# Contrast adjustment on one Trainium2 core: the means moved from ScalarE to VectorE and TensorE, tiles moved as whole rows, and the first store held until the fifth load

## The chip, the core and the metric

The kernel runs on one core of a Trainium2 chip. The core has five engines that run side by side: TensorE (PE in the profile), VectorE (DVE), ScalarE (ACT), GpSimd (POOL) and SyncE (SP). Data move between the memory (HBM) and the on-chip SBUF by 16 DMA engines; a transfer is issued by an instruction on an engine's queue, here SP for loads and ACT for stores. The metric is the device time of one execution in microseconds (us); lower is better.

## What is computed

`x` holds 16 x 3 images of 512 x 512 numbers in f32, 50.33 MB; the output has the same shape. Each image is stretched around its own mean by a factor of 1.5 and clipped to 0..1.

```python
def reference(x, factor):
    mean = np.mean(x, axis=(2, 3), keepdims=True)
    return np.clip(mean + factor * (x - mean), 0, 1).astype(np.float32)
```

An image has to be read as a whole before its first output number is known. The kernel writes `mean + factor * (x - mean)` as `factor * x + bias`, with `bias = (1 - factor) * mean`.

## The kernel before

The input is cut into 12 tiles of 128 partitions by 8192 columns (4.19 MB each). One row of 8192 numbers is 32 KB, an image fills 32 rows, so a tile holds four whole images. The tiles go through `ring`, an SBUF buffer with six places (`BUFS`): tile t uses place t % 6, is loaded into it, clipped in place, and stored from it. Tile t + 6 can be loaded into the place only when the store of tile t has read it out.

The order on each engine is the program's order: the main block runs under a manual schedule, and what is planned on one engine stays in the sequence in which it is written. Semaphores between engines and transfers are set by the framework from the tiles that are read and written.

Per tile:
- `load` (L74, on SP's queue) brings it in. Tiles 0 and 1 come alone, tiles 2 and 3 in one transfer, tiles 4 and 5 in one transfer; from tile 6 on they come one by one, each issued behind the store of the tile six before it.
- `add` (L89, ScalarE) copies the tile onto itself and sums each row into a column of `sums`. A table has to be loaded for it once. For tile 0 the sum is divided: ScalarE sums columns 4352 to 8191, VectorE the first 4352 (L108).
- `shift_by` (L94, TensorE) multiplies `sums` with `blockw`, a 128 x 128 matrix of four 32 x 32 blocks filled with (1 - factor) / pixels. One matmul with one column adds the 32 rows of each image and leaves the bias in every row of a PSUM tile, `bias`.
- `clip` (L78 and L82, VectorE) does `x * factor + bias`, and then max with 0 and min with 1, two instructions over the tile.
- `store` (L99, on ACT's queue) writes it out. Tile 0 is clipped and stored in three pieces of 1024, 2048 and 5120 columns (`CUTS`), so that stores can begin early; the others go as one transfer.

The loop sets what stands behind what on ACT's queue: the sum of tile t + 1 is written ahead of the store of tile t.

```python
        for t in range(1, n_tiles):
            shift_by(t, own)
            clip(t, 0, ROW)
            if t + 1 < n_tiles:
                own = add(t + 1)
            store(t, 0, ROW)
            if t + BUFS < n_tiles:
                load(t + BUFS)
```

Of the kernel before, what the change touches and what calls it, by code (L numbers as in the profile page):

```python
# [1 line left out]

# [4 lines left out]


P = 128  # L10
ROW = 8192
BUFS = 6
CUTS = (0, 1024, 3072, ROW)
SUM = 4352


@with_exitstack
def kernel(
    ctx: ExitStack,
    tc: tile.TileContext,  # L20
    x: bass.AP,
    factor: float,
    out: bass.AP,
):

    nc = tc.nc
    f32 = mybir.dt.float32
    Alu = mybir.AluOpType  # L30
    Act = mybir.ActivationFunctionType

    B, C, H, W = x.shape
    n_img, n_pix = B * C, H * W
    ppi = n_pix // ROW
    per_tile = P // ppi
    n_tiles = n_img // per_tile
    assert ppi * ROW == n_pix and per_tile * n_tiles == n_img

    factor = float(factor)  # L40
    wconst = (1.0 - factor) / float(n_pix)

    x_f = x.rearrange("b c h w -> (b c h w)")
    out_f = out.rearrange("b c h w -> (b c h w)")

    def dram(ap, t, c0=0, c1=ROW):
        return bass.AP(tensor=ap.tensor, offset=t * P * ROW + c0, ap=[[ROW, P], [1, c1 - c0]])

    consts = ctx.enter_context(tc.tile_pool(name="consts", bufs=1))
    xpool = ctx.enter_context(tc.tile_pool(name="xpool", bufs=1))  # L50
    small = ctx.enter_context(tc.tile_pool(name="small", bufs=1))
    psum = ctx.enter_context(tc.tile_pool(name="psum", bufs=1, space=bass.MemoryType.PSUM))


    sums = small.tile([P, 2 * n_tiles], f32, name="sums")
    bias = psum.tile([P, n_tiles], f32, name="bias")

    blockw = consts.tile([P, P], f32, name="blockw")
    nc.gpsimd.memset(blockw, 0.0)  # L59
    for a in range(0, P, ppi):  # L60
        nc.gpsimd.memset(blockw[a : a + ppi, a : a + ppi], wconst)  # L61


    ring = xpool.tile([P, BUFS, ROW], f32, name="ring")

    def load(t, c0=0, c1=ROW, n=1):

        b = t % BUFS
        src = bass.AP(
            tensor=x_f.tensor,  # L70
            offset=t * P * ROW + c0,
            ap=[[ROW, P], [P * ROW, n], [1, c1 - c0]],
        )
        nc.sync.dma_start(out=ring[:, b : b + n, c0:c1], in_=src)  # L74

    def clip(t, c0, c1):
        part = ring[:, t % BUFS, c0:c1]
        nc.vector.tensor_scalar(  # L78
            out=part, in0=part, scalar1=factor, scalar2=bias[:, t : t + 1],
            op0=Alu.mult, op1=Alu.add,  # L80
        )
        nc.vector.tensor_scalar(  # L82
            out=part, in0=part, scalar1=0.0, scalar2=1.0, op0=Alu.max, op1=Alu.min
        )

    def add(t, c0=0):
        part = ring[:, t % BUFS, c0:ROW]
        own = sums[:, 2 * t : 2 * t + 1]
        nc.scalar.activation(out=part, in_=part, func=Act.Copy, accum_out=own)  # L89
        return own  # L90

    def shift_by(t, *parts):
        for k, part in enumerate(parts):
            nc.tensor.matmul(  # L94
                bias[:, t : t + 1], blockw, part, start=k == 0, stop=k == len(parts) - 1
            )

    def store(t, c0, c1):
        nc.scalar.dma_start(out=dram(out_f, t, c0, c1), in_=ring[:, t % BUFS, c0:c1])  # L99

    with tc.manual_schedule():
        load(0)
        load(1)
        load(2, n=2)
        load(4, n=2)

        rest = sums[:, 1:2]
        nc.vector.tensor_reduce(  # L108
            out=rest, in_=ring[:, 0, 0:SUM], axis=mybir.AxisListType.X, op=Alu.add
        )  # L110
        shift_by(0, add(0, SUM), rest)
        for c0, c1 in zip(CUTS[:-2], CUTS[1:-1]):
            clip(0, c0, c1)
            store(0, c0, c1)
        clip(0, CUTS[-2], ROW)
        own = add(1)
        store(0, CUTS[-2], ROW)
        load(BUFS)
        for t in range(1, n_tiles):
            shift_by(t, own)  # L120
            clip(t, 0, ROW)
            if t + 1 < n_tiles:
                own = add(t + 1)
            store(t, 0, ROW)
            if t + BUFS < n_tiles:
                load(t + BUFS)


# [1 line left out]
_INS = ['x', 'factor']  # L130
_OUTS = [((16, 3, 512, 512), 'float32')]

_NUMBERS = {'factor': 1.5}


# [26 lines left out]
```

## Time and profile before

| | us |
|---|---|
| median of 3 runs | 239.19 (239.05 to 239.28) |
| the profiled execution: its span, first to last instruction | 237.8 |
| around the span (median less span) | 1.4 |
| VectorE busy | 112.1 |
| ScalarE busy | 82.9 |
| TensorE busy | 7.6 |

The page gives the profiled execution by its span; its time outside of the span isn't given apart, and the row around the span compares it with the median of the runs. The kernel reads 50.33 MB and writes 50.33 MB, 423 GB/s over the span.

Lines of the profile are read so: in the slices, the span is cut into 40 equal parts and each digit is the busy share of a part in tenths. A group has its line in the kernel, engine, operation, output <- input with partitions x columns and type, how often; then the busy time and the mean ns of one; then the idle time of the engine ahead of them and who ended it. A wait line has who waited for whom, us in total, times, and the longest. In a window the engines stand in the order PE, PEld (weight loads), DVE, ACT, POOL, each with busy us and instructions, then the granted TensorE clock, the busy share of the DMA engines and GB/s. The trace also keeps a record of each packet that a DMA engine moved: queue, start, duration and bytes; one row of a tile is one packet.

### The profile page before, as it was taken

What the parts mean: (1) busy time and instruction counts of PE and PEld (TensorE: products, weight loads), DVE (VectorE), ACT (ScalarE), POOL (GpSimd) and SP (SyncE); (2) the same over time, 40 slices, a digit from 0 to 9 for tenths busy, and PEclk for the clock granted to TensorE, in tenths of its full rate; (3) what the DMA queues carried; (4) which work ended last, traced back from release to release, by engine and by line L of the source; (5) the groups of instructions that cost most, each with busy time, mean ns of one, the idle gap of its engine ahead of it and who ended that gap; (6) DMA issues with size and microseconds to landing.
All of it is one profiled execution on the core that took longest, in us unless ns stands there. A gap on an engine that the chain in (4) does not pass through costs nothing.

```text
span 237.8 us, 219 instructions
## 1 busy us (share of the span) xinstructions
PE 7.6 (3%) x26; PEld 6.5 (3%) x26; DVE 112.1 (47%) x29; ACT 82.9 (35%) x25; POOL 0.9 (0%) x9
## 2 busy tenths in 40 slices
PE   0010000000000000000000000000000000000000
PEld 0000000000000000000000000000000000000000
DVE  0078786009990039979407705902920950770000
ACT  2051900399000697380091083056038009100000
POOL 1000000000000000000000000000000000000000
DMA  7999999999999999999999999999999999999996
GB/s 265 441 441 442 401 471 429 391 413 430 457 441 435 413 408 430 435 435 441 441 441 441 441 435 435 402 419 430 435 441 441 441 441 441 441 430 413 413 430 259
DMA packets 3712, 100.66 MB, mean 423 GB/s; under 512 B 384, under 2 KB 384, under 8 KB 512
## 3 DMA queue, kind: packets, MB, share of 16 engines
q1 hardware_dynamic: 1696, 50.33, 49.6%
q10 hardware_dynamic: 2016, 50.33, 49.1%
HBM read 50.33 MB, written 50.33 MB: 423 GB/s over the span
## 4 chain that ended last, share of the span: by engine, by line
DMA 52%; another core or an unknown queue 15%; DVE 11%; issue 9%; PE 1%; ACT 1%; SPq 0%; ACTq 0%
DMA ring<-in_x_dram 33%; DMA out_dram<-ring 20%; DVE ring L78 6%; DVE ring L82 6%; PE bias L94 1%; ACT ring L89 1%; SPq L74 0%; ACTq L99 0%; ACTq L89 0%
## 5 line engine op out<-in xcount | busy, mean ns | idle before, releaser
L89 ACT ACTIVATE ring<-ring 128x8192 f32<-128x8192 f32 (+1 forms) x12 | 80.7, 6725 | 119.4 <-DMA ring<-in_x_dram 119.4
L78 DVE TENSOR_SCALAR ring<-ring,bias 128x8192 f32<-128x8192 f32 (+3 forms) x14 | 54.3, 3880 | 87.1 <-PE bias L94 87.1
L82 DVE TENSOR_SCALAR ring<-ring 128x8192 f32<-128x8192 f32 (+3 forms) x14 | 53.4, 3817 | 0.5
L94 PE MATMUL bias<-sums,blockw 128*128 128x1 f32 x26 | 7.6, 361 | 196.1 <-ACT ring L89 195.6
L94 PEld LDWEIGHTS bias<-sums,blockw 128*128 128x128 f32 x26 | 6.5, 311 | 197.1 <-ACT ring L89 179.9
L108 DVE TENSOR_REDUCE sums<-ring 128x1 f32<-128x4352 f32 x1 | 4.7, 4686 | 13.0 <-DMA ring<-in_x_dram 13.0
L89 ACT ACTIVATION_READ_ACCUMULATOR ring<-ring 128x1 f32 x12 | 2.2, 186 | 0.0
L89 ACT ACT_TABLE_LOAD x1 | 1.3, 1283 | 0.7 <-PEq L143 0.7
L61 POOL MEMSET blockw<- 32x32 f32 x4 | 0.5, 116 | 0.2
L59 POOL MEMSET blockw<- 128x128 f32 x1 | 0.2, 205 | 0.3 <-POOLq L143 0.3
L143 POOL MEMSET const-bfloat16-1.0<- 128x1 bf16 x1 | 0.1, 111 | 0.0
L143 POOL MEMSET const-uint8-127<- 128x1 uint8 x1 | 0.1, 111 | 0.0
L143 POOL MEMSET const-float32-1.0<- 128x1 f32 x1 | 0.1, 108 | 0.0
L143 POOL MEMSET const-float32-0.0<- 128x1 f32 x1 | 0.1, 103 | 0.2 <-issue 0.2
## 6 DMA issues: line engine op xcount, KB each, us to landing
out_dram<-ring ACTq DMA_DIRECT2D x11, 4096.0 KB, 44.2
ring<-in_x_dram SPq DMA_DIRECT2D x8, 4096.0 KB, 33.3
ring<-in_x_dram SPq DMA_DIRECT2D x2, 8192.0 KB, 60.6
out_dram<-ring ACTq DMA_DIRECT2D x1, 2560.0 KB, 37.5
out_dram<-ring ACTq DMA_DIRECT2D x1, 1024.0 KB, 25.9
out_dram<-ring ACTq DMA_DIRECT2D x1, 512.0 KB, 16.1
```

Of the source, the lines that this page charges most:

```text
L59: nc.gpsimd.memset(blockw, 0.0)
L61: nc.gpsimd.memset(blockw[a : a + ppi, a : a + ppi], wconst)
L78: nc.vector.tensor_scalar(out=part, in0=part, scalar1=factor, scalar2=bias[:, t : t + 1], op0=Alu.mult, op1=Alu.add,)
L82: nc.vector.tensor_scalar(out=part, in0=part, scalar1=0.0, scalar2=1.0, op0=Alu.max, op1=Alu.min)
L89: nc.scalar.activation(out=part, in_=part, func=Act.Copy, accum_out=own)
L94: nc.tensor.matmul(bias[:, t : t + 1], blockw, part, start=k == 0, stop=k == len(parts) - 1)
L108: nc.vector.tensor_reduce(out=rest, in_=ring[:, 0, 0:SUM], axis=mybir.AxisListType.X, op=Alu.add)
L143: nc = _bacc.Bacc("TRN2", target_bir_lowering=False, num_devices=1)
```

## The change

- ScalarE computes nothing and loads no table. Its queue has the 12 stores only.
- `head` (VectorE) sums the first 4096 columns of a tile into `sums`. `shift` (TensorE) multiplies `blockw` with the other 4096 columns in eight matmuls of 512 columns, all accumulated in one PSUM tile `acc` (two buffers), and adds the product with `sums` to its first column. VectorE then sums `acc` over its 512 columns into `bias`, now in SBUF.
- Every tile is loaded and stored as one transfer of 128 rows of 32 KB. SP's first six instructions are the loads of tiles 0 to 5, with no wait.
- Tile 0 is clipped up to column 7680, then tile 1 is summed and clipped. Then VectorE sums the first 512 columns of tile 4 (`begun`), for which it must wait until the fifth load has landed, and only then clips the last 512 columns of tile 0. The store of tile 0 waits for that piece, and the other stores follow it on the same queue.
- From then on, each turn of the loop sums and clips tile t on VectorE and TensorE, stores it, and issues the load of tile t + 6.

The core of the diff:

```diff
-CUTS = (0, 1024, 3072, ROW)
-SUM = 4352
+BLK = 512
+HEAD = 4096
...
-    bias = psum.tile([P, n_tiles], f32, name="bias")
+    bias = small.tile([P, n_tiles], f32, name="bias")
...
+    def head(t, k=0, c0=0, c1=HEAD):
+        own = sums[:, 2 * t + k : 2 * t + k + 1]
+        nc.vector.tensor_reduce(
+            out=own, in_=ring[:, t % BUFS, c0:c1], axis=mybir.AxisListType.X, op=Alu.add
         )
+        return own
...
+    def shift(t, *heads):
+
+        acc = psum.tile([P, BLK], f32, name="acc")
+        for c0 in range(HEAD, ROW, BLK):
+            nc.tensor.matmul(
+                acc, blockw, ring[:, t % BUFS, c0 : c0 + BLK], start=c0 == HEAD, stop=False
+            )
+        for own in heads:
+            nc.tensor.matmul(acc[:, 0:1], blockw, own, start=False, stop=own is heads[-1])
+        nc.vector.tensor_reduce(
+            out=bias[:, t : t + 1], in_=acc, axis=mybir.AxisListType.X, op=Alu.add
+        )
...
-    def add(t, c0=0):
-        part = ring[:, t % BUFS, c0:ROW]
-        own = sums[:, 2 * t : 2 * t + 1]
-        nc.scalar.activation(out=part, in_=part, func=Act.Copy, accum_out=own)
-        return own
+    with tc.manual_schedule():
+        for t in range(BUFS):
+            load(t)
...
+        gate = BUFS - 2
+        shift(0, head(0))
+        clip(0, 0, ROW - BLK)
+        shift(1, head(1))
+        clip(1)
+        begun = head(gate, 0, 0, BLK)
+        clip(0, ROW - BLK, ROW)
+        for t in range(n_tiles):
+            if t == gate:
+                shift(t, begun, head(t, 1, BLK, HEAD))
+            elif t > 1:
+                shift(t, head(t))
+            if t > 1:
+                clip(t)
+            store(t)
             if t + BUFS < n_tiles:
                 load(t + BUFS)
```

More of the change, by code (lines that the diff above doesn't have):

```diff
@@ L30 @@
     Alu = mybir.AluOpType
-    Act = mybir.ActivationFunctionType
     B, C, H, W = x.shape
@@ L37 @@
     n_tiles = n_img // per_tile
-    assert ppi * ROW == n_pix and per_tile * n_tiles == n_img
+    assert ppi * ROW == n_pix and per_tile * n_tiles == n_img and n_tiles > BUFS
     factor = float(factor)
@@ L44, with dram @@
     out_f = out.rearrange("b c h w -> (b c h w)")
-    def dram(ap, t, c0=0, c1=ROW):
-        return bass.AP(tensor=ap.tensor, offset=t * P * ROW + c0, ap=[[ROW, P], [1, c1 - c0]])
+    def dram(ap, t):
+        return bass.AP(tensor=ap.tensor, offset=t * P * ROW, ap=[[ROW, P], [1, ROW]])
     consts = ctx.enter_context(tc.tile_pool(name="consts", bufs=1))
@@ L51 @@
     small = ctx.enter_context(tc.tile_pool(name="small", bufs=1))
-    psum = ctx.enter_context(tc.tile_pool(name="psum", bufs=1, space=bass.MemoryType.PSUM))
+    psum = ctx.enter_context(tc.tile_pool(name="psum", bufs=2, space=bass.MemoryType.PSUM))
     sums = small.tile([P, 2 * n_tiles], f32, name="sums")
-    bias = psum.tile([P, n_tiles], f32, name="bias")
+    bias = small.tile([P, n_tiles], f32, name="bias")
     blockw = consts.tile([P, P], f32, name="blockw")
@@ L64, with load, store, clip @@
     ring = xpool.tile([P, BUFS, ROW], f32, name="ring")
[L66 to L72, printed above, removed]
-        )
-        nc.sync.dma_start(out=ring[:, b : b + n, c0:c1], in_=src)
-    def clip(t, c0, c1):
+    def load(t):
+        nc.sync.dma_start(out=ring[:, t % BUFS, :], in_=dram(x_f, t))
+    def store(t):
+        nc.scalar.dma_start(out=dram(out_f, t), in_=ring[:, t % BUFS, :])
+    def head(t, k=0, c0=0, c1=HEAD):
+        own = sums[:, 2 * t + k : 2 * t + k + 1]
+        nc.vector.tensor_reduce(
+            out=own, in_=ring[:, t % BUFS, c0:c1], axis=mybir.AxisListType.X, op=Alu.add
+        )
+        return own
[10 more added lines that the diff above has]
+        )
+    def clip(t, c0=0, c1=ROW):
         part = ring[:, t % BUFS, c0:c1]
@@ L84, in clip @@
         )
-    def add(t, c0=0):
-        part = ring[:, t % BUFS, c0:ROW]
-        own = sums[:, 2 * t : 2 * t + 1]
-        nc.scalar.activation(out=part, in_=part, func=Act.Copy, accum_out=own)
-        return own
[L92 to L99, printed above, removed]
-    with tc.manual_schedule():
[L102 to L124, printed above, removed]
+    with tc.manual_schedule():
+        for t in range(BUFS):
[15 more added lines that the diff above has]
+            store(t)
             if t + BUFS < n_tiles:
```

## The prediction

> **What bounds the kernel now.** I read the page from the slices (part 2) to the chain (part 4) and the groups (part 5), then the waits by engine, busy time in chosen windows, the timeline, and last the trace's records of single DMA packets.
>
> ```profile
> span 237.8 us, 219 instructions
> ...
> PE 7.6 (3%) x26; PEld 6.5 (3%) x26; DVE 112.1 (47%) x29; ACT 82.9 (35%) x25; POOL 0.9 (0%) x9
> ...
> DMA  7999999999999999999999999999999999999996
> ...
> DMA packets 3712, 100.66 MB, mean 423 GB/s; under 512 B 384, under 2 KB 384, under 8 KB 512
> ...
> DMA 52%; another core or an unknown queue 15%; DVE 11%; issue 9%; PE 1%; ACT 1%; SPq 0%; ACTq 0%
> ```
>
> No engine is busy for half of the span, and the DMA row is 9 in every slice but the two at the ends. The 26% that the chain gives to DVE, issue, PE and ACT is a path through the waits; transfers run beside all of it. So the kernel is bound by 100.66 MB and by the rate at which the 16 DMA engines take it.
>
> ```profile
> 5.00:20.00 15.00, 1.14 (x4) 1.00 (x4) 6.28 (x4) 3.50 (x2) 0.00 (x0) 1.00 1.00 433
> ```
>
> This is the busy time in a window of pure loading (after the times: PE, PEld, DVE, ACT, POOL, granted clock, DMA share, GB/s). 433 GB/s is a plateau: by packet records spread over their durations, 5 us bins give 432 to 434 for pure loads (5 to 25 us), loads and stores mixed (55 to 195) and pure stores (195 to 235). A 32 KB packet takes 1.213 us (median), and each DMA engine has 50.33 x 2 MB / 16 / 32768 B = 192 of them to carry: 192 x 1.213 = 232.9 us. The first packet starts at 1.76, the last ends at 236.64, and 1.1 us follow. So on the engine that ends last, 234.9 - 232.9 = 2.0 us are all that a change of order can win. A bubble, in which neither queue has a packet, is all that it can newly lose.
>
> Those 2.0 us, from the packet records (sums over 16 engines, divided by 16):
> - the opening packets, 1.6 to 2.06 us in place of 1.213: 0.58 us. They stay.
> - short rows of the first tile's three stores: 4 KB packets take 0.159 us, 8 KB 0.309, 20 KB 0.761. Per engine 8 x (0.159 + 0.309 + 0.761) = 9.83 against 8 x 1.213 = 9.70: 0.13 us.
> - some 60 load packets of 1.24 to 1.85 us, nearly all starting between 35 and 54 us: 0.71 us. The bins there are 417, 422, 420, 409 GB/s. Elsewhere after the opening such packets cost 0.04 us in all.
> - one engine falls behind in that stretch and stays there: at the end 15 engines stop by 235.88 and the last at 236.64, 0.76 later. After the second load its lag was 0.05.
> (Packets overlap slightly, 16.05 in flight, which gives back some 0.6.)
>
> **The change part by part.** All prices below are against the profiled span of 237.8 us. The median of the runs is 239.19, so 1.4 us lie around the span; I carry these 1.4 over.
>
> ```profile
> L89 ACT ACTIVATE ring<-ring 128x8192 f32<-128x8192 f32 x11 | 77.3, 7027 | 108.4 <-DMA ring<-in_x_dram 108.4
> L78 DVE TENSOR_SCALAR ring<-ring,bias 128x8192 f32<-128x8192 f32 x11 | 49.4, 4490 | 86.4 <-PE bias L94 86.4
> L82 DVE TENSOR_SCALAR ring<-ring 128x8192 f32<-128x8192 f32 x11 | 48.7, 4427 | 0.4
> L94 PE MATMUL bias<-sums,blockw 128*128 128x1 f32 x26 | 7.6, 361 | 196.1 <-ACT ring L89 195.6 <-DVE sums L108 0.5
> ...
> L108 DVE TENSOR_REDUCE sums<-ring 128x1 f32<-128x4352 f32 x1 | 4.7, 4686 | 13.0 <-DMA ring<-in_x_dram 13.0
> ```
> ```profile
> SPq L74 <- DMA out_dram<-ring: 157.5, 8, 33.3
> ```
>
> The groups with shapes kept apart give the unit prices; the last line, from SP's waits, says that loads from the seventh on wait for stores to land.
>
> 1. ScalarE's sums go: 7.03 + 0.19 us a tile, and the table load of 1.28 us. None was on the DMA's path, as the transfers ran beside them: worth 0. Stores no longer queue behind an ACTIVATE on ACT: store 1, ready at 39.5, was issued at 45.65 because the sum of tile 2 (waiting for the joint load of 2 and 3) stood ahead. Other transfers were in flight, so that too is 0.
>
> 2. VectorE gets 4096 columns of sum: 4686 / 4352 = 1.077 ns a column, 4.4 us. It also gets a 512-column sum from PSUM, not in this trace: nearest row 512 x 1.077 = 0.55, ends 0.5 and 1.2; I take 0.6. With the two clips (8.92) and the small matmul's 0.6 between, 14.6 us a tile when data wait. A tile needs 8.39 MB / 433 = 19.4 us of DMA. Spare, 4.8 us a tile: cost 0.
>
> 3. TensorE gets eight 128x512 f32 matmuls a tile, of which no row exists. Each f32 matmul shows as two records; the pair with one column takes 0.59, which sets a floor of 8 x 0.59 = 4.7 us. The nearest row in columns is the weight load: two of 128 columns start 0.167 us apart, 1.3 ns a column. At that pace 512 columns in two records take 1.34 us, a tile 10.7; if each record passes its columns twice, 21.4. I take 10.7, the value with no further assumption, and keep 4.7 and 21.4.
> The Trainium skill prices it otherwise: its page FP8 and Floating Point Precision (TensorE Precision Notes) gives true f32 four passes, and TensorE: Matmul & The Clock Gate (Part 1) gives 2.4 GHz warm and 1.2 GHz after idling. An estimate from both is 8 x 4 x 512 columns = 6.8 us warm, 13.7 cold; the sum comes out the same by either. No row here shows such a matmul, and the granted clock of 1.00 stands beside an almost idle PE.
>
> 4. The gate. Loads 0 to 5 are issued at once; at 433 GB/s each takes 9.7 us, landing at 12.7, 22.4, 32.1, 41.8, 51.5, and the sixth, if alone, at 61.2. VectorE and TensorE do tiles 0 and 1 meanwhile: sum 0 by 24.9 (13.0 + 10.7 + 0.6 + 0.6), the first 7680 columns' clip (8.4) to 33.3, head 1 to 37.7, its matmul and reduction to 38.9, clip 1 to 47.9. The added wait is on VectorE, `begun`, for load 4. Behind it stand the last 512 columns of tile 0's clip (2 x 0.46, from 757 and 1285 ns for 1024 and 2048 columns), all of tiles 2 to 11, and so store 0 and every store behind it on ACT's queue. It ends at 51.8 + 0.6 + 0.9 = 53.3. The cover is load 5: until 61.2 the DMA has work without any store, 7.9 us of cover. The first store before showed its first packet 3.6 us after its issue, behind loads in flight; so store 0 starts at 57 and nothing is idle. Without the cover each us of delay would cost one.
>
> 5. After it. Load 5 and store 0 share the rate until 65.4, store 0 lands at 71, and load 6 starts some 2 us later. Store 1 waits on ACT's queue from 53.4, and store 2 is ready at 67.6 (head 4.4, 1.2, clip 8.9 after 53.3), so stores run alone at 433 meanwhile, as they did from 195 us on. From there VectorE offers a store each 14.6 us and the queue takes one each 19.4, so a store always waits; load t+6 needs store t landed, and load 7 is issued near 88 while load 6 runs to 94. Loads end near 191 (before 194.3), the last tile is ready at 191 + 10.7 + 1.2 + 8.9 = 212, and its turn on the queue comes at 225: 13 us spare.
>
> 6. Whole rows. The short-row loss of 0.13 goes. The slow packets have one trait that I can use: they lie where small-row stores met the two-tile loads. Whole-row stores beside single-tile loads, from 78 us on, lost under 0.03 us in 116. That is the nearest row for the new mixture, so I let the 0.71 go. Its bounds are 0 won and 0.71 won. Of the lagging engine's 0.76, which arose with them, I take 0.3, ends 0 and 0.76.
>
> Sum: 0.13 + 0.71 + 0.3 = 1.1 us. Span 237.8 - 1.1 = 236.7, time 239.19 - 1.1 = **238.1**. The ends: gains from 0.1 to 1.6, 237.6 to 239.1.
>
> **Rivals.**
> (a) The slow packets come whatever the rows: the 4 KB packets ran from 23 to 34 us without them, and 20 KB packets from 55 to 64 too, which speaks for another cause, such as the first mixing of reads and writes. Then only 0.13 is won, less what the new mixture loses: 239.1, from 238.7 to 239.6. The Trainium skill has a rule that would leave as little: HBM Reference, Specifications, puts a core alone near 425 GB/s, and the kernel's mean is 423. The trace disagrees, with 433 for 15 us in a row.
> (b) TensorE becomes the bound, the case on the slower side. Its place is the eight matmuls ahead of each bias, its price x us a tile. The last tile's store would be issued at 13 + 12 x + 10.7 (small matmul, PSUM sum, clip), and end some 11.7 later (9.7 of packets, 2 of start and finish): 35.4 + 12 x. It reaches 237.8 at x = 16.9; below that nothing shows, at 18 the span is 251.4 and the time 252.8, at 21.4 the time is 294. The gate's cover ends near the same x: store 0 goes out at 13 + 2x + 11.8, so past 61 from x = 18. For it: 21.4 is within my bounds; against it: that needs two passes at the slow pace with nothing overlapped.
> (c) The whole mixed stretch runs like 35 to 54, because TensorE's 2 MB of reads a tile or the one-tile queues slow the packets: 0.71 us per 19 over 55 to 191 is 5.1, so 239.19 - 1.1 + 5.1 = 243.2. Against it, ScalarE read and wrote whole tiles before, with no such packets after 61 us.
>
> **How the numbers follow.** Forecast 0.57, (a) 0.23, (b) 0.10, (c) 0.10. 0.2% is 0.5 us, about what a measurement of this kernel can tell. The forecast's own range is 237.6 to 238.6. Faster: 0.56, nearly all of the forecast. Same: 0.20, most of (a). Slower: 0.24, (b), (c) and the rest of (a). The range of 237.5 to 240 holds the forecast and (a), and leaves out (b) and (c), 0.20 together.
>
> **What would show it.** Right: bins near 433 from 5 us to the end, 16 packets in flight throughout, store 0 issued at 53 to 54 and load 6 at 71 to 73, no load packet group above 1.24 us, DVE ahead of the stores from 80 us on. Wrong: a DMA slice under 9 near 60 us (gate), PE busy above 17 us a tile (b), GB/s bins of 410 to 425 (a, c), or an engine whose last packet ends well after the others.

## The result and the profile after

The changed kernel takes 240.33 us (median of 6 runs), the kernel before 239.12 (median of 6): a ratio of 1.006, interval 1.0046 to 1.0074. It is slower by some 1.2 us, where 1.1 faster was forecast, so 2.2 us lie between the predicted 238.1 and the measured time.

The page of the changed kernel; the rows answer to those shown of the kernel before, and PEclk is the granted clock of TensorE in tenths of full speed.

```profile
span 238.4 us, 594 instructions
...
PE 113.8 (48%) x218; PEld 49.7 (21%) x218; DVE 167.8 (70%) x51; POOL 0.9 (0%) x9
...
PEclk9999975865685988979687589569559659855555
DMA  7999999999999999999999999999999999999995
GB/s 269 440 434 440 440 440 429 434 434 357 434 423 434 434 429 412 440 443 434 440 434 434 429 434 429 434 429 429 423 434 440 440 440 429 434 440 429 429 440 220
DMA packets 3457, 100.68 MB, mean 422 GB/s; under 512 B 384, under 2 KB 384, under 8 KB 384
...
q8 instruction: 1, 0.02, 0.0%
```

The DMA is still full from end to end, at the same mean rate. Two things are new. The tenth slice has 357 GB/s, and a third queue, q8, moved one packet of kind "instruction", 0.02 MB. TensorE's row suggests what is fetched: 218 matmul and 218 weight-load records, where there were 26 of each. I call such a packet, which brings instructions while the program runs, a refill.

In the packet records (as in the prediction, lost time is summed over the 16 engines and divided by 16):

| us | before | after |
|---|---|---|
| first packet starts | 1.76 | 1.74 |
| opening packets, lost an engine | 0.58 | 0.70 |
| load packets slowed near the first stores, lost an engine | 0.71 (35 to 54 us) | 1.03 (54 to 57 us) |
| short rows, lost an engine | 0.13 | 0 |
| mean end of the 16 engines | 235.75 | 236.18 |
| end of the last engine | 236.64 | 237.19 |
| instruction packets after the start | none | 16 KB at 106.28 for 0.88 us, and at 239.31 |

The packet at 106.28 occupies one of the 16 DMA engines. The load packet that starts at 107.16 behind it takes 1.753 us in place of 1.213. Together 0.88 + 0.54 = 1.42 us fall on that one engine. Joining each packet to the one that ends where it starts gives each of the 16 engines its 192 rows. By these chains the engine of the refill was 0.28 us ahead of the mean of the 16 before it, 1.05 behind after it, and 1.02 behind at the end: the lag isn't made up. It ends at 237.19, and the second-last engine at 236.61. So 0.58 of the 1.42 us reach the end of the run; nearly all of the rest, 0.81, is what that engine had been ahead of the one that was last until then.

The gate, in windows of the changed kernel (columns PE, PEld, DVE, POOL, granted clock, DMA share, GB/s) and in its timeline:

```profile
50.00:54.00 4.00, 0.00 (x0) 0.00 (x0) 2.04 (x4) 0.00 (x0) 0.50 0.99 426
54.00:58.00 4.00, 0.14 (x1) 0.15 (x1) 3.80 (x1) 0.00 (x0) 0.50 0.98 311
58.00:62.00 4.00, 4.00 (x7) 1.93 (x8) 3.49 (x2) 0.00 (x0) 0.50 1.04 451
```
```profile
51.93 0.69 DVE L69 TENSOR_REDUCE sums<-ring 128x1 f32<-128x512 f32 x1 [4.74 <-DMA ring<-in_x_dram]
...
53.05 0.43 DVE L93 TENSOR_SCALAR ring<-ring 128x512 f32<-128x512 f32 x1
53.39 4.41 DVE L69 TENSOR_REDUCE sums<-ring 128x1 f32<-128x4096 f32 x1
53.51 0.86 ACTq L65 DMA_DIRECT2D out_dram<-ring  x2
```

The first line of the timeline is `begun`, released by the fifth load; stores 0 and 1 go out at 53.51 (predicted 53.3). DMA share stays at 0.98 from 54 to 58 while GB/s falls to 311: the engines were never idle, but 29 load packets took up to 2.67 us. The first store packet starts at 57.84. So the drop is slowness of packets, not a bubble.

**The baseline.** Every run comes with its span. The kernel before, in the rounds of the experiments, has spans near 237.2 with 239.0 us: some 1.75 lie around the span. The two executions with a span of 237.8 took 239.56 and 239.57 in one set. So the profile that the prediction started from was of an execution some 0.6 longer than the usual one, and no execution on record has as little as 1.4 around its span (the least is 1.73). From the usual 237.2 to 238.4 the span alone holds nearly the whole loss; around it lie 1.87 us in the profiled execution of the changed kernel (240.27).

### The profile page after: what moved, and what is told of

Same layout as the page of the kernel before. It is cut to its first block, busy times and chain, and to the rows that moved or that the text cites. A ratio compares the mean times of both kernels' runs of the same rounds, so it can differ in the third digit from the quotient of the medians.

```text
span 238.4 us, 594 instructions
## 1 busy us (share of the span) xinstructions
PE 113.8 (48%) x218; PEld 49.7 (21%) x218; DVE 167.8 (70%) x51; POOL 0.9 (0%) x9
## 4 chain that ended last, share of the span: by engine, by line
DMA 51%; DVE 16%; another core or an unknown queue 16%; PE 4%; SPq 1%; issue 0%
DMA ring<-in_x_dram 32%; DMA out_dram<-ring 19%; DVE ring L89 6%; DVE ring L93 6%; DVE sums L69 4%; PE acc L78 4%; SPq L62 1%; DVE bias L83 1%; PE acc L82 1%
## 5 line engine op out<-in xcount | busy, mean ns | idle before, releaser
L78 PE MATMUL acc<-ring,blockw 128*128 128x512 f32 x192 | 109.9, 737 | 45.0 <-DMA ring<-in_x_dram 45.0
L78 PEld LDWEIGHTS acc<-ring,blockw 128*128 128x128 f32 x192 | 45.0, 241 | 100.8 <-issue 100.8
L69 DVE TENSOR_REDUCE sums<-ring 128x1 f32<-128x4096 f32 (+2 forms) x13 | 53.1, 4085 | 17.8 <-DMA ring<-in_x_dram 17.8
L89 DVE TENSOR_SCALAR ring<-ring,bias 128x8192 f32<-128x8192 f32 (+2 forms) x13 | 54.0, 4158 | 0.4
L93 DVE TENSOR_SCALAR ring<-ring 128x8192 f32<-128x8192 f32 (+2 forms) x13 | 53.3, 4098 | 0.4
L82 PE MATMUL acc<-sums,blockw 128*128 128x1 f32 x26 | 5.7, 287 | 43.2 <-DVE sums L69 43.2
L83 DVE TENSOR_REDUCE bias<-acc 128x1 f32<-128x512 f32 x12 | 8.3, 691 | 25.2 <-PE acc L82 25.2
L82 PEld LDWEIGHTS acc<-sums,blockw 128*128 128x128 f32 x26 | 5.5, 245 | 51.5 <-DVE sums L69 49.1
```

The source lines that it names most:

```text
L69: nc.vector.tensor_reduce(out=own, in_=ring[:, t % BUFS, c0:c1], axis=mybir.AxisListType.X, op=Alu.add)
L78: nc.tensor.matmul(acc, blockw, ring[:, t % BUFS, c0 : c0 + BLK], start=c0 == HEAD, stop=False)
L82: nc.tensor.matmul(acc[:, 0:1], blockw, own, start=False, stop=own is heads[-1])
L83: nc.vector.tensor_reduce(out=bias[:, t : t + 1], in_=acc, axis=mybir.AxisListType.X, op=Alu.add)
L89: nc.vector.tensor_scalar(out=part, in0=part, scalar1=factor, scalar2=bias[:, t : t + 1], op0=Alu.mult, op1=Alu.add,)
L93: nc.vector.tensor_scalar(out=part, in0=part, scalar1=0.0, scalar2=1.0, op0=Alu.max, op1=Alu.min)
```

## The experiments

Theory 1 came from the table above: TensorE's longer program needs refills, and a refill makes one DMA engine late. Theory 2, the rival: the held stores, with the slow packets at 54 us, carry the loss. All ratios are to the kernel before in the same set (238.95 to 239.07 us).

| run | us | ratio (95% interval) | instruction packets after the start |
|---|---|---|---|
| e1_two_matmuls | 245.40 | 1.0269 (1.0255 to 1.0283) | none |
| e2_before_more_matmuls | 240.16 | 1.0049 (1.0034 to 1.0064) | 95.1 |
| e3_no_gate | 240.56 | 1.0071 (1.0055 to 1.0086) | 130.4, 240.6 |
| e4_scalar_sums | 239.21 | 1.0014 (1.0002 to 1.0025) | none |
| e5_before_few_more | 239.92 | 1.0032 (1.0020 to 1.0044) | 238.9 |
| e6_no_gate_three | 243.79 | 1.0205 (1.0188 to 1.0223) | 223.2 |
| e7_before_whole_rows | 239.80 | 1.0035 (1.0016 to 1.0053) | none |
| e8_early_small_store | 239.89 | 1.0034 (1.0022 to 1.0046) | none |
| e9_scalar_sums_eight_more | 240.97 | 1.0078 (1.0062 to 1.0094) | 80.8, 239.6 |
| e10_scalar_sums_two_more | 239.41 | 1.0019 (1.0008 to 1.0029) | none |
| e11_scalar_sums_later | 239.81 | 1.0029 (1.0019 to 1.0039) | none |
| e12_before_single_loads | 250.10 (see below) | 1.0385 (1.0336 to 1.0435) | none |
| e13_one_big_matmul | 239.89 | 1.0035 (1.0022 to 1.0048) | 8 KB at 204.1 |
| e14_one_big_many_small | 240.70 | 1.0074 (1.0060 to 1.0089) | 91.5, 8 KB at 204.1, 239.2 |

**e1_two_matmuls**, to the changed kernel:
```diff
-HEAD = 4096
+HEAD = 7168
```


> The changed kernel with 7168 columns of each tile summed on VectorE and 1024 on TensorE: two big matmuls a tile in place of eight, 37 matmuls in all in place of 109. Theory 1 (instruction refills: TensorE's longer program is fetched during the run by one DMA engine in a 16 KB packet of 0.88 us at 106 us, which makes that engine the last, and again at the end of the run at 239.3 us): no packet of the instruction queue after the start, last engine no longer 0.58 us behind the second-last, less around the span; time about 239.2, 1.1 below the changed kernel. Theory 2 (the gate: the load packets slowed to 1.3 to 2.7 us from 54.3 to 57.0 us when the held stores are issued cost 1.03 us an engine and carry the loss): 240.3, unchanged. VectorE needs 17.9 us a tile against 19.4 of DMA, so neither theory expects a cost from there.

Measured 245.40, which neither theory allowed. The slices and a window (columns as above):

```profile
DMA  7999999999999999999999999999999999999096
```
```profile
226.00:233.00 7.00, 0.00 (x0) 0.00 (x0) 5.72 (x2) 0.00 (x0) 0.50 0.17 75
```

The 0 in the DMA row is a bubble of some 6 us: VectorE still clips the last tile until 231.8. My bound was wrong. VectorE is held until 53 and has ten tiles to do by 226, when the last store's turn comes: (226 - 53) / 10 = 17.3 us a tile, not 19.4. It needed 17.9. No refill came with 37 matmuls, but the run doesn't tell the theories apart.

**e2_before_more_matmuls**, to the kernel before, after each bias matmul:
```diff
+        for _ in range(8):
+            nc.tensor.matmul(spare, blockw, parts[0], start=True, stop=True)
```


> The kernel before with eight more matmuls of one column a tile into a spare PSUM column, 109 matmuls as in the changed kernel; they add instructions and no data, and their result is not used. Theory 1 (instruction refills): instruction packets of 16 KB appear during the run and at its end, time about 240.2, 1.1 above the kernel before, of which 0.5 outside of the span. Theory 2 (the gate): within 0.2 us of the kernel before, 239.1.

Measured 240.16, 1.2 above the kernel before, as theory 1 said. Its page:

```profile
PE 48.6 (20%) x218; PEld 47.5 (20%) x218; DVE 112.1 (47%) x29; ACT 82.9 (35%) x25; POOL 0.9 (0%) x9
...
q8 instruction: 1, 0.02, 0.0%
```

The same 218 records as the changed kernel, the same kind of packet (16 KB, 0.885 us, at 95.06), and nothing else of the change: no gate, no whole rows, no new sums. The last engine ends at 236.72, 0.59 behind the second-last. The refill at the run's end wasn't in this profile; the other runs' spans are 238.2 to 238.4.

**e3_no_gate**, to the changed kernel:
```diff
-        clip(0, 0, ROW - BLK)
-        shift(1, head(1))
-        clip(1)
-        begun = head(gate, 0, 0, BLK)
-        clip(0, ROW - BLK, ROW)
+        clip(0)
...
-            if t == gate:
-                shift(t, begun, head(t, 1, BLK, HEAD))
-            elif t > 1:
-                shift(t, head(t))
-            if t > 1:
+            if t > 0:
+                shift(t, head(t))
                 clip(t)
```


> The changed kernel without the wait for the fifth load: tile 0 is clipped whole and stored when ready, near 34 us, tile 1 near 49. Theory 1 (instruction refills): refills stay, so the time stays above 239.6; the slow load packets of 54 to 57 us become fewer or move, worth 0 to 1.0 us: 239.6 to 240.3. Theory 2 (the gate): the slow packets go and the loss with them, 239.1 or less.

Measured 240.56, a little above what theory 1 allowed, and against theory 2. Without the hold the loss stays, and so do the slow packets: 21 load packets from 33 to 36 us, 0.65 us an engine, just ahead of the first store's packets at 37.0. They come with the first stores, wherever these are put.

**e4_scalar_sums**: the changed kernel's transfers and hold, its sums replaced.
```diff
-            elif t > 1:
-                shift(t, head(t))
...
+        nc.scalar.activation(out=part, in_=part, func=Act.Copy, accum_out=own)
...
+        nc.tensor.matmul(
+            bias[:, t : t + 1], blockw, sums[:, 2 * t : 2 * t + 1], start=True, stop=True
+        )
```


> The changed kernel's transfers (six single loads at once, whole rows, first store held until the fifth load) with the sums back on ScalarE: one matmul of one column a tile, 12 in all, and the table load. Theory 1 (instruction refills): no refill, time about 239.2, as the slow packets at the gate stay (about 1.0 us an engine) and replace those that the kernel before had (0.7). Theory 2 (the gate): 240.3, as the changed kernel.

Measured 239.21, as theory 1 said: the transfers of the changed kernel cost 0.2 us of the 1.2 to 1.4, with 0.75 us an engine of slow packets at 55 to 59 us. These alone can make an engine late: in the profiled execution (239.72, above the median) the last engine ends 0.79 behind the second-last, without a refill.

**e5_before_few_more**: as e2, `range(3)` in place of `range(8)`.

> The kernel before with three more matmuls of one column a tile in place of eight: 49 matmuls, fewer than the about 55 after which the refill came in the runs so far. Theory 1 (one refill packet, a step): no instruction packet after the start, time within 0.2 us of the kernel before, 239.0. Rival (each added instruction costs something of its own, in proportion): 36 of 96 matmuls, so 0.4 to 0.5 us above the kernel before, 239.4.

Measured 239.92, missed by both. The page and the packet records show why.

```profile
span 237.0 us, 364 instructions
...
PE 23.0 (10%) x98; PEld 21.9 (9%) x98; DVE 112.1 (47%) x29; ACT 82.9 (35%) x25; POOL 0.9 (0%) x9
```

The span is 237.0 to 237.2 in all five runs, no longer than before: 36 added matmuls cost nothing inside, which goes against a price for each. But a 16 KB packet at 238.89, for 1.35 us, comes behind the end of the span, and the time around the span grows from 1.75 to 2.5 to 3.0. A refill behind the last instruction can thus cost outside of the span. It need not: the changed kernel's profiled execution has one at 239.31 and 1.87 around its span.

**e6_no_gate_three**: e3 with `HEAD = 6656`.

> The changed kernel without the wait for the fifth load and with three big matmuls a tile (6656 columns on VectorE, 1536 on TensorE), 48 matmuls in all. VectorE needs 17.3 us a tile and starts at 13, so the last tile is ready near 221, before its turn on the queue. Theory 1 (refill): no refill, 239.0 to 239.3. Rival (the loss comes from TensorE's and VectorE's sums or from the whole-row transfers themselves): 240.3 or more, as with eight matmuls.

Measured 243.79, inconclusive for its question. A refill came after all, at 223.2, with 48 matmuls. Slow packets, moreover, return near the end of each store, 31 to 193 us, 4.0 us an engine in all. What makes these packets slow isn't shown.

**e7_before_whole_rows**, to the kernel before:
```diff
-CUTS = (0, 1024, 3072, ROW)
+CUTS = (0, ROW)
...
-        load(2, n=2)
-        load(4, n=2)
+        load(2)
+        load(3)
+        load(4)
+        load(5)
```


> The kernel before with its sums on ScalarE as they were, but six single loads ahead and tile 0 stored in one piece: whole rows alone, no held store. If short rows and double loads cost what the prediction took for them (0.13 for the rows, 0.71 for the slow packets), 238.1 to 238.9. If the slow load packets come with the first stores whatever their rows (in all six profiles so far, 0.65 to 1.03 us an engine), 238.8 to 239.1: only the 0.13 goes.

Measured 239.80, 0.7 above the kernel before and above both expectations. The slow packets are there (29 to 33 us, 1.0 us an engine). The loads also end late: the last load's last packet is through at 207.3 us, against 194.3 in the kernel before and 191.4 in the changed one. The last tile was therefore ready at 225.7, too late for the queue, which lost some 0.3 us. In e12 below, which stores tile 0 in pieces, the loads end at 206.7, so this goes with the single loads and not with the whole rows. Here the hold has its use: with it and the same single loads, e4 has its last load in at 191.

**e8_early_small_store**, to e7:
```diff
+        nc.scalar.dma_start(
+            out=bass.AP(tensor=out_f.tensor, offset=0, ap=[[ROW, P], [1, P]]), in_=blockw
+        )
```


> The kernel of whole rows on ScalarE's sums, and one store of 128 short rows (512 bytes each, from the weights, overwritten by tile 0's store later) as the first instruction on the store queue, near 1 to 2 us. If the slow load packets are the price of the store queue's first use, they move to the opening and are gone near 30 us: 0 to 0.8 below the kernel of whole rows without it. If they are the price of the first whole-tile stores beside loads, they stay near 30 us and the time is 0 to 0.2 above it.

Measured 239.89, equal to e7; the slow packets stay at 29 to 31 us. They are not the price of the queue's first use.

**e9_scalar_sums_eight_more** and **e10_scalar_sums_two_more**: e4 with
```diff
+        for _ in range(8):    # e10: range(2)
+            nc.tensor.matmul(
+                spare, blockw, sums[:, 2 * t : 2 * t + 1], start=True, stop=True
+            )
```


> The changed kernel's transfers with the sums on ScalarE (239.2 before), and eight more matmuls of one column a tile into a spare PSUM column, 108 in all; their result is not used. Theory 1 (the length of TensorE's program, through refills): 240.2 to 240.6, which is the changed kernel's time without any of its sums on TensorE or VectorE. Rival (the sums themselves, their reads of SBUF or VectorE's load, cost the 1.2 us): 239.2, as without the added matmuls.

> The same with two more matmuls a tile, 36 in all, fewer than the 37 that ran without any refill packet. Theory 1 (a step at a refill): no instruction packet after the start, 239.0 to 239.4. Rival (in proportion to the instructions added): 24 of 96 of 1.2, so 0.3 above the 239.2 of no added matmuls: 239.5.

Measured 240.97 and 239.41. The pages of e9 and then e10:

```profile
PE 47.9 (20%) x216; PEld 47.0 (20%) x216; DVE 107.7 (45%) x27; ACT 86.7 (36%) x25; POOL 0.9 (0%) x9
...
q8 instruction: 1, 0.02, 0.0%
```
```profile
PE 17.2 (7%) x72; PEld 16.2 (7%) x72; DVE 107.7 (45%) x27; ACT 86.8 (36%) x25; POOL 0.9 (0%) x9
```

With 36 matmuls no packet came, and the interval overlaps that of e4; but 239.41 lies between the two expectations, 239.4 and 239.5, and doesn't part a step from a price for each. That is left to e5's unchanged span. With 108 the refills came and the time rose by 1.6, more than the 1.0 to 1.4 expected: the changed kernel's loss without its sums.

**e11_scalar_sums_later**, to e4:
```diff
-            out=sums[:, 1:2], in_=ring[:, gate, 0:BLK], axis=mybir.AxisListType.X, op=Alu.add
+            out=sums[:, 1:2], in_=ring[:, gate, 0:4096], axis=mybir.AxisListType.X, op=Alu.add
```


> The changed kernel's transfers with the sums on ScalarE, and the first store held 3.9 us longer: VectorE's sum over tile 4 ahead of the last piece of tile 0 takes 4096 columns in place of 512 (its result is not used), so that the store goes out near 57.5, when less than half of the sixth load is left. If the slow load packets (0.75 us an engine in the run with 512 columns) are the price of the first stores beside loads in flight, fewer load packets are left to slow, and the time falls by 0 to 0.5 to 238.7 to 239.2. If the DMA runs dry before the first store arrives, near 61, it rises by the gap. If neither, 239.2.

Measured 239.81, 0.6 above e4, with no gain. The slow packets moved to 58 to 60 us with the stores and cost 0.8 us an engine all the same. Where the 0.6 comes from isn't shown; its profiled execution was the shortest of the set.

**e12_before_single_loads**, the second hunk of e7 alone.

> The kernel before with tiles 2 to 5 loaded by four single transfers; tile 0 is still stored in three pieces. If joining two tiles in one transfer makes the slow load packets of 35 to 54 us, they go: 238.2 to 238.6. If they come with the first stores, they stay: within 0.2 us of the kernel before, 239.0.

Measured 250.10, with six runs scattered from 246.1 to 254.2; the ratio in the table rests on the three shortest (246.1, 248.9 and 249.7) and stands for 9.2 us. Either is far from both expectations. The slices, and windows with columns PE, PEld, DVE, ACT, POOL, granted clock, DMA share, GB/s:

```profile
DMA  7999999999999999999999999999999999999920
```
```profile
230.00:238.00 8.00, 0.00 (x0) 0.00 (x0) 0.00 (x0) 0.00 (x0) 0.00 (x0) 1.00 0.80 344
238.00:248.00 10.00, 0.00 (x0) 0.00 (x0) 0.00 (x0) 0.00 (x0) 0.00 (x0) 1.00 0.11 49
```

From 238 on 0.11 of the DMA is busy, some two engines of sixteen. They carry the last packets until 246.6, about 9 us behind the rest, and slow packets come by twos from 70 to 190 us. So single loads with tile 0's pieces, and no hold, make two engines run late. Why is open.

**e13_one_big_matmul** and **e14_one_big_many_small**: the changed kernel with its hold, whole rows and VectorE's sums, and most of TensorE's columns given to ScalarE.
```diff
+TAIL = 4608
...
-        for c0 in range(HEAD, ROW, BLK):
+        for c0 in range(HEAD, TAIL, BLK):
...
+        part = ring[:, t % BUFS, TAIL:ROW]
+        nc.scalar.activation(out=part, in_=part, func=Act.Copy, accum_out=own)
...
+        for _ in range(6):    # e14 alone
+            nc.tensor.matmul(spare, blockw, heads[-1], start=True, stop=True)
```


> The changed kernel with its held store, whole rows and eight-into-one sums, but 3584 of TensorE's 4096 columns a tile summed by ScalarE: one big matmul a tile in place of eight, 37 matmuls in all, and VectorE's share unchanged at 4096 columns. Theory 1 (refills of TensorE's program): no instruction packet after the start, 239.1 to 239.5, as with the sums wholly on ScalarE. Rival (VectorE's sums, the PSUM reduction or the held store carry the changed kernel's loss): 240.2 or more, since all three are still there.

> The same with six matmuls of one column a tile added into a spare PSUM column, 109 in all as in the changed kernel; their result is not used. Theory 1 (refills): instruction packets during the run and near its end, 0.8 to 1.5 us above the kernel with 37, so 240.0 to 240.9. Rival (TensorE's 512-column reads of the tiles cost it, not the length of its program): as the kernel with 37.

Measured 239.89 and 240.70. The pages of e13 and then e14:

```profile
span 237.8 us, 345 instructions
...
PE 36.2 (15%) x74; PEld 17.4 (7%) x74; DVE 167.8 (71%) x51; ACT 40.7 (17%) x25; POOL 0.9 (0%) x9
...
q14 instruction: 1, 0.01, 0.0%
```
```profile
PE 66.8 (28%) x218; PEld 48.0 (20%) x218; DVE 167.9 (70%) x51; ACT 40.7 (17%) x25; POOL 0.9 (0%) x9
...
q8 instruction: 1, 0.02, 0.0%
q14 instruction: 1, 0.01, 0.0%
```

The two differ by 72 matmuls of one column that nobody reads, and by 0.8 us, the lower end of what theory 1 said. But e13 lies between the two expectations, 0.7 above e4. Part of that is around its span, 2.0 against 1.75; another instruction packet, of 8 KB and on a queue of its own (q14), came at 204 us in both; it took 0.31 us, and the row behind it 1.57. What else the 0.7 holds isn't shown. Nor does e13 give the changed kernel's loss back: with 37 matmuls in place of 109 it is only 0.4 below the changed kernel's 240.33.

## Why the prediction was wrong

**The step that failed is part 3, TensorE.** It priced "eight 128x512 f32 matmuls a tile" by the time that they run, found it hidden, and put 0. They were hidden: a tile's eight take 10.0 us in the first burst against 10.7 taken. What it left out is that 109 matmuls in place of 13 have to be fetched, and that the fetch uses the resource which bounds the kernel. Adding matmuls of one column alone cost 1.2 us (e2 to before), 1.6 (e9 to e10) and 0.8 (e14 to e13), mean 1.2. By e5 that is a step, not a price for each: with 74 matmul records or fewer no 16 KB packet came, with 96 and 98 one, near the end; with 216 or 218 one in the run and most times one behind it. That TensorE owns the packets of q8 is inferred from this count. It isn't the number of all instructions: e13, with 345, has no 16 KB packet, and e6, with 344, has one.
The Trainium skill states the refill: Runtime: NRT & Kernel Launch, Terms, gives each engine an instruction memory refilled in blocks of 16 KiB. The traces agree, with 16384 bytes in 0.88 us.
How the refill costs is shown in part. The engine that took it is the last to end in the changed kernel, e2, e3 and e9, by 0.58 to 0.99 us, which is part of the 1.2; in e14 another engine is the last. Where the rest of a refill's cost arises isn't shown. Nor is the refill the whole of the changed kernel's loss, as e13 shows, with 0.85 above the kernel before and no 16 KB packet.

**Part 6 failed too, by its nearest row.** "So I let the 0.71 go": the slow packets came in every run, 0.5 to 1.0 us an engine near the first stores, and 1.03 in the changed kernel. Rival (a) had these packets right, though not the time. The 0.13 for short rows went as said, and was outweighed. The 0.3 for the lagging engine was taken from an execution that had it; in e5's profile, with before's transfers, the last engine is 0.01 behind and the span 237.0. The gain of 1.1 rested on these two, so none of it came. Set against that profile of e5, the 16 engines of the changed kernel end 0.55 later in the mean (236.18 to 235.63), and its last engine 1.01 behind the mean in place of 0.24.

**Baseline:** "1.4 us lie around the span" compared one execution's span with another's time. It is 1.75. Two figures of the prediction are off without consequence: by the line that it shows, the chain gives DVE, issue, PE and ACT 11 + 9 + 1 + 1 = 22%, not 26%, and store 2's terms add up to 67.8, not 67.6.

What held: VectorE's turn is 14.7 us a tile (53.39 to 68.07; predicted 14.6), and its PSUM sum 0.69 (0.6). Part 4's store 0 at 53.5 (53.3) and part 5's last load packet at 191.4 (191) agree; load 6 started at 75.99, not 73, without cost. Part 1's zero is not shown alone. Groups of the changed kernel, shapes kept apart:

```profile
L78 PE MATMUL acc<-ring,blockw 128*128 128x512 f32 x192 | 109.9, 737 | 45.0 <-DMA ring<-in_x_dram 45.0
...
L69 DVE TENSOR_REDUCE sums<-ring 128x1 f32<-128x4096 f32 x11 | 48.5, 4413 | 13.1 <-DMA ring<-in_x_dram 13.1
...
L83 DVE TENSOR_REDUCE bias<-acc 128x1 f32<-128x512 f32 x12 | 8.3, 691 | 25.2 <-PE acc L82 25.2
```

Rival (b), TensorE as the bound, didn't come: 10 us a tile stays far under 16.9. In the first burst weight loads, one to a record, first start 0.85 us apart and later 0.43, as two pairs of the timeline show:

```profile
14.16 0.34 PEld L78 LDWEIGHTS acc<-ring,blockw 128*128 128x128 f32 x1 [0.52 <-issue]
15.02 0.34 PEld L78 LDWEIGHTS acc<-ring,blockw 128*128 128x128 f32 x1 [0.52 <-issue]
...
19.62 0.19 PEld L78 LDWEIGHTS acc<-ring,blockw 128*128 128x128 f32 x1 [0.24 <-issue]
20.05 0.19 PEld L78 LDWEIGHTS acc<-ring,blockw 128*128 128x128 f32 x1 [0.24 <-issue]
```

Two records a matmul make 1.71 us and then 0.86. In the second burst the granted clock can be read beside it: 0.50 while weight loads start 0.85 apart (38.33 to 42.60), and 1.00 while they start 0.43 apart (from 43.22). The windows, in the columns of the gate:

```profile
38.00:42.50 4.50, 4.50 (x6) 1.69 (x5) 4.46 (x2) 0.00 (x0) 0.50 0.96 415
43.50:46.00 2.50, 2.50 (x7) 1.14 (x6) 2.50 (x1) 0.00 (x0) 1.00 1.00 433
```

Ahead of 19.09 us the trace has no record of the clock, and a window shows 1.00 there although the first burst runs at the slow pace; the trace of the kernel before has no such record at all. So the 1.00 that the prediction set beside an almost idle PE was no reading of the clock. The estimate from the Trainium skill's FP8 and Floating Point Precision and TensorE: Matmul & The Clock Gate was 13.7 / 8 = 1.71 and 6.8 / 8 = 0.85: the trace agrees, and better than with my row.
Rival (c), a slow mixed stretch, didn't come in the changed kernel (433 GB/s of rows in the bins from 60 to 190 us, but one of 425 at the refill). e6 and e12 have slow stretches of this kind, though their cause isn't shown.

What stays open: why load packets slow near the first stores; the part of a refill's cost that isn't on its engine; the 0.7 us between e4 and e13; the two late engines of e12. None of the runs beat the kernel before.

## What to carry to other kernels

In a kernel whose DMA engines are full, count instructions as transfers: here 109 matmuls in place of 13 brought 16 KB packets onto a DMA engine that holds rows of the tiles, and the last engine sets the end. Before taking a profile's losses for gains, compare its span with those of several executions; what a single one lost may not be there to win. And when a wait holds an engine back, its later allowance is the time that remains, divided by what remains.

## What was not expected of the hardware

- One 16 KB instruction packet lasts 0.88 us where a 32 KB tile row lasts 1.21, and slowed the row behind it by 0.54 (0.4 in e2, e3, e9 and e14).
- The time around the span is not constant: 1.75 us, and 2.5 to 3.0 in e5, whose refill falls behind the last instruction.
- Replacing two joint loads by four single ones cost some 9 us through two late DMA engines (e12), with the same bytes and the same program otherwise.
